# Normalising the mixer input half by half, putting an attention head first, and planning the issue order with other durations, in a fused decoder layer

## The chip, the cores and the metric

The program runs on one core of a Trainium2 chip. The metric is device time in microseconds (us) of one execution; lower is better. The core has five engines with in-order instruction queues: TensorE (PE in the profile, with its weight loads as PEld), VectorE (DVE), ScalarE (ACT), GpSimd (POOL) and SyncE (SP, which here only issues DMAs). They meet only through semaphores. A measurement of this kernel can tell a change from none at about 0.5% of its time.

## What is computed

One inference step of a hybrid decoder layer on 544 tokens (512 of a prompt, 32 of eight samples), width 1024, in float32:

```python
x = x + 0.5 * swiglu(rms(x, norm_ffn1))                  # feed-forward block 1
h = rms(x, norm_mix)                                     # the mixer input
qa, ka, va, qkv_b, z_b, b_b, a_b, gate = split(h @ w_in) # one wide projection
o_a = merged_attention(qa, ka, va)                       # 12 heads in 3 groups (dilation 1, 4, 16)
o_b = gated_deltanet(qkv_b, z_b, b_b, a_b)               # 8 heads, conv of width 4, chunked delta rule
gt  = sigmoid(gate)
x = x + (gt_a * (o_a @ w_proj_a) + gt_b * (o_b @ w_proj_b)) @ w_out
x = x + 0.5 * swiglu(rms(x, norm_ffn2))                  # feed-forward block 2
y = rms(x, norm_out)
```

`rms(x, w) = x * rsqrt(mean(x*x) + 1e-6) * w`. Keys, values, conv rows and delta-net states are outputs too.

## The kernel before

**Layout and units.** Activations lie transposed: 8 tiles of 128 features by 544 tokens. Tokens are worked in two halves of 272, called h = 0 and 1. The work on PE is a list of *units* (`make_plan`, L155). A unit is one column block of a weight matrix times one half: for the wide projection 8 weight tiles, and for each three matmuls of 128x272, since a float32 product is made of split halves: weight-high x input-high, weight-high x input-low, weight-low x input-high (`unit`, L612). So a unit of the mixer has 24 matmuls. The split of the input is a pair of tiles named `xh` and `xl`, that of a weight group `G`.

**The mixer's order.** After feed-forward block 1 come two units `ba`, then the list `MIX_ORDER` (L43): `("p", k)` is delta-net head k (query, key, value: 6 units), `("a", k)` an attention head (6 units), `z` the delta-net's output gate (2 units each), `t` the branch gates (4 units each). After the list come the projections `pa` and `pb`.

**The norm factor.** The mixer's input needs a factor r per token that is known only after the whole of x is known and ACT and POOL have summed its squares. The kernel starts the mixer without it: the first units multiply x times the norm weight, without r, and each result is multiplied by r when DVE takes it out of PSUM (`take`, L870). Meanwhile a generator `renorm` (L561) makes normalised tiles `xn2` for all 544 tokens: per tile one DVE multiply (name `xt`), one ACT copy (`xh`), one DVE subtraction (`xl`). From unit `first_ba + NORMED` on (L38, L687) the units use these, and ACT takes their results out of PSUM. `renorm` is started when the second half's factor is there (`norm_fin`, L601).

**Side work and the planner.** All that is not a unit (conv, the delta-net pair of heads `gdn_pair`, its sample part, attention per slot `attn_slot`, `attn_sample`, `z_fin`, `fin_a`, the norm) is a Python generator. While the program is written, `pump` (L646) runs after every third matmul of a unit and lets each generator go on for one step if the planner's clock says its operands are there. That clock is `Meter` (L48): it adds up an assumed duration for each recorded instruction, engine by engine and for the DMA queue (L75 to L93). Nothing of this runs on the chip; it fixes only the order in each engine's queue. When a unit needs something that is not there yet (a buffer, a conv before it, a loaded tile), `until` and `force` (L292, L666) run side work alone until it is. The names that matter below: `ob`, the delta-net output of a head, stored to DRAM (`od`) and loaded again for `z_fin` (L824); `oad` and `oA`, the attention output stored and loaded again by `fin_a` (L849) for `pa`; `av`, an attention head's projected values; `g`, the decay of the delta-net, made by `gating` (L954), with `gc`, `gm` and `LB`/`LA` beside it; `convout`, the conv states, loaded at the start of the mixer (L774).

Of the kernel before, what the change touches and what calls it, by code (L numbers as in the profile page):

```python
# [37 lines left out]
NORMED = 10  # L38
# [4 lines left out]
MIX_ORDER = [("p", 0), ("p", 1), ("a", 0), ("p", 2), ("a", 1), ("p", 3), ("a", 2), ("a", 3), ("p", 4), ("a", 4), ("p", 5), ("a", 5)]  # L43
# [4 lines left out]
class Meter:  # L48
# [10 lines left out]
    def note(self, eng, op, args, kw):  # L59
# [201 lines left out]
class Builder:  # L261
# [299 lines left out]
    def renorm(self):  # L561

        ts = []

        def finish():
            t, (hi, lo) = ts.pop(0), self.xn2[-1 - len(ts)]
            self.tt(lo, t, hi, ALU.subtract)
            self.free(1)

        for n in range(KT):  # L570
            yield from self.need(3)
            t = self.S(name="xt")
            self.stt(t, self.x[n], self.wn[1][:, n:n + 1], self.rr, ALU.mult, ALU.mult)
            if ts:
                finish()
            yield "scalar"
            self.xn2.append((self.S(dt=F32R, name="xh"), self.S(dt=F32R, name="xl")))
            self.act(self.xn2[-1][0], t, AF.Copy)
            ts.append(t)
            t = None  # L580
            yield "vector"
        finish()
        self.renormed = True

    def norm_fin(self, h):
# [15 lines left out]
        elif h == 1 and self.in_mix:  # L601
            self.spawn(self.renorm())
# [77 lines left out]
    def kernel_units(self):  # L680
# [4 lines left out]
        first_ba = next(i for i, u in enumerate(self.units) if u[0] == "ba")  # L685
        for ui, u in enumerate(self.units):
            self.prefetch(ui)  # L687
            if ui == first_ba + NORMED:
                self.until(lambda: self.renormed)
                self.xn, self.xn2, self.normed = self.xn2, None, True  # L690
                self.free(2 * KT)
# [78 lines left out]
    def enter_mix(self):  # L770
# [5 lines left out]
        self.xn2, self.renormed, self.normed = [], False, False  # L776
        self.live = 16 + 1 + 2 + KT
# [18 lines left out]

    def u_ba(self, h, wids):
# [8 lines left out]
    def u_z(self, n, h, wids):  # L806
# [4 lines left out]
        ps, s = self.unit(wids, self.xn, h), self.sl(h)  # L811
# [1026 lines left out]
```

## Time and profile before

| | us |
|---|---|
| three timed runs | 1721.02, 1719.72, 1713.33 (median 1719.72) |
| the profiled execution | 1718.26 |
| its span, first to last instruction | 1716.5 |
| PE busy / DVE busy / ACT busy | 1648.8 / 1010.2 / 618.8 |

The span has three parts: feed-forward block 1 to about 414 us, the mixer to about 1280 us, feed-forward block 2 to the end. A timeline row gives start, duration, engine, operation, written tile and read tiles, and in brackets the idle time of the engine before it with what ended it. Matmuls overlap: what counts is the distance of their starts. "PEclk" is the granted TensorE clock as a share of full speed: 1.00 stands for 2.4 GHz, 0.50 for 1.2 GHz.

### The profile page before, as it was taken

The page shows a single profiled execution, that of the slowest core. Times are in us where ns is not written, and L with a number is a line of the kernel's source. Part 1 is how long each engine was busy: PE and PEld are TensorE (multiplying, and loading weights), DVE is VectorE, ACT ScalarE, POOL GpSimd, SP SyncE. Part 2 cuts the span into 40 slices and gives each one's busy share as a digit, 9 for nine tenths or more (in the row PEclk, how much of TensorE's full clock was granted, in tenths as well). Part 3 has the DMA queues.
Part 4 walks back from the last instruction along what each step waited for, and adds up shares of the span by engine and source line. Part 5 has one row for each costly group of instructions (what it writes and reads, how often), then busy time and mean ns, then how long its engine had stood idle before and what let it go on. Part 6 is the DMA issues. An engine that isn't in the chain of part 4 may idle for free.

```text
span 1716.5 us, 33595 instructions
## 1 busy us (share of the span) xinstructions
PE 1648.8 (96%) x13373; PEld 1603.2 (93%) x13373; DVE 1010.2 (59%) x2460; ACT 618.8 (36%) x1548; POOL 169.0 (10%) x289
## 2 busy tenths in 40 slices
PE   7999999999699998998999979999999999999997
PEld 7999999999599978997999978999999999999997
DVE  7754255545867857876866566353356654255534
ACT  5332232332344424553433425332233332223332
POOL 5000000011111211221021111000011000000012
PEclk9999999999899999998999979999999999999999
DMA  5223222221334454564445756433242223223221
GB/s 178 86 87 99 86 83 90 87 81 58 125 99 141 150 185 119 176 199 128 160 151 180 253 160 193 142 111 90 94 140 88 87 87 93 92 75 99 87 75 65
DMA packets 116433, 205.12 MB, mean 120 GB/s; under 512 B 30962, under 2 KB 57108, under 8 KB 116276
## 3 DMA queue, kind: packets, MB, share of 16 engines
q1 hardware_dynamic: 104708, 162.43, 29.7%
q0 software_dynamic: 10992, 39.99, 7.8%
q8 instruction: 105, 1.72, 0.4%
q10 hardware_dynamic: 576, 0.56, 0.1%
q14 instruction: 52, 0.43, 0.1%
HBM read 172.20 MB, written 30.73 MB: 118 GB/s over the span
## 4 chain that ended last, share of the span: by engine, by line
PE 85%; DVE 7%; DMA 4%; ACT 1%; issue 1%; SPq 0%; DVEq 0%; POOL 0%; ACTq 0%
PE mm L122 43%; PE sd L122 42%; DVE R L122 1%; DMA md<-ast 1%; DVE H L122 1%; DVE y L122 1%; DMA ob<-od 1%; DVE G L122 1%; DMA st<-in_ssm_dram 1%; DVE xl L122 1%; DVE r L122 1%; DMA cache<-in_kc_dram 0%; ACT s L122 0%; SPq L122 0%; DMA raw<-in_W_dram 0%
## 5 line engine op out<-in xcount | busy, mean ns | idle before, releaser
L122 PE MATMUL mm<-xh,G 128*128 128x272 f32 x3632 | 744.3, 296 | 9.0 <-ACT xh L122 3.1
L122 PEld LDWEIGHTS mm<-xh,G 128*128 128x128 f32 x3632 | 590.8, 191 | 27.8 <-issue 13.2
L122 PE MATMUL mm<-xl,G 128*128 128x272 f32 x1816 | 527.6, 291 | 8.5 <-DVE xl L122 8.5
L122 DVE TENSOR_TENSOR G<-raw,G 128x512 fp32r<-128x512 f32 x468 | 303.9, 691 | 180.3 <-ACT G L122 174.7
L122 PE MATMUL sd<-xh,G 128*128 128x272 f32 x1904 | 362.5, 288 | 0.0
L122 PEld LDWEIGHTS mm<-xl,G 128*128 128x128 f32 x1816 | 347.0, 191 | 10.5 <-DVE xl L122 9.8
L122 ACT ACTIVATE G<-raw 128x512 fp32r<-128x512 f32 x474 | 272.1, 622 | 101.5 <-PE mm L122 47.3
L122 PEld LDWEIGHTS sd<-xh,G 128*128 128x128 f32 x1904 | 300.2, 188 | 0.2
L122 PE MATMUL sd<-xl,G 128*128 128x272 f32 x952 | 273.6, 287 | 0.0
L122 PEld LDWEIGHTS sd<-xl,G 128*128 128x128 f32 x952 | 179.0, 188 | 0.1
L122 PE MATMUL sd<-hh,G 128*128 128x272 f32 x1287 | 163.2, 288 | 0.0
L122 PEld LDWEIGHTS sd<-hh,G 128*128 128x128 f32 x1287 | 161.9, 188 | 0.1
L122 POOL TENSOR_TENSOR acc<-acc,H 128x272 f32<-128x272 f32 x55 | 44.5, 810 | 909.9 <-ACT H L122 908.9
L122 ACT ACTIVATE hh<-H 128x272 fp32r<-128x272 f32 x88 | 38.0, 432 | 201.8 <-DVE H L122 201.8
L122 PE MATMUL mm<-hh,G 128*128 128x272 f32 x825 | 104.7, 288 | 0.0
L122 PEld LDWEIGHTS mm<-hh,G 128*128 128x128 f32 x825 | 103.8, 188 | 0.0
L122 ACT ACTIVATE H<-H 128x272 f32<-128x272 f32 (+1 forms) x89 | 38.2, 429 | 161.2 <-DVE H L122 161.2
L122 POOL DMA_DIRECT2D raw<-in_W_dram x76 | 41.7, 549 | 519.9 <-DVE G L122 283.1
L122 DVE SCALAR_TENSOR_TENSOR H<-H,H 128x272 f32<-128x272 f32 x120 | 55.7, 465 | 30.7 <-ACT H L122 30.2
L122 DVE SCALAR_TENSOR_TENSOR x<-sd,x 128x272 f32<-128x272 f32 x49 | 21.5, 439 | 78.2 <-PE sd L122 78.2
L122 DVE TENSOR_TENSOR hh<-H,hh 128x272 fp32r<-128x272 f32 x88 | 39.0, 443 | 43.8 <-ACT hh L122 43.8
L122 DVE SCALAR_TENSOR_TENSOR y<-U,vec,y 128x568 f32<-128x568 f32 x72 | 62.1, 863 | 3.8 <-ACT y L122 1.9
(261 smaller groups left out, 1763.2 us busy)
## 6 DMA issues: line engine op xcount, KB each, us to landing
raw<-in_W_dram SPq DMA_DIRECT2D x161, 512.0 KB, 3.5
raw<-in_W_dram POOLq DMA_DIRECT2D x76, 512.0 KB, 4.2
qkv<-qd SPq DMA_DIRECT2D x36, 256.0 KB, 5.0
st<-in_ssm_dram SPq DMA_DIRECT2D x32, 256.0 KB, 4.8
cache<-in_kc_dram SPq DMA_DIRECT2D x28, 256.0 KB, 3.8
cache<-in_vc_dram SPq DMA_DIRECT2D x28, 256.0 KB, 4.5
qd<-av SPq DMA_DIRECT2D x24, 256.0 KB, 3.0
out_dram<-av SPq DMA_DIRECT2D x24, 256.0 KB, 3.1
```

Source lines behind the costliest of these rows:

```text
L122: r = f(*args, **kw)
```

## The change

The mixer input is normalised in halves: `renorm(h)` is started as soon as that half's factor is there, works on 128x272, and units switch to the normalised tiles for half 0 from unit 8 and for half 1 from unit 9 (before: both from 10). `MIX_ORDER` begins with an attention head, `("a", 0)`, which stood third. `Meter` gets other numbers: DMA issue to start 1.6 for 1.1 us and 250 for 358 GB/s, a matmul 0.011 + 0.00042 for 0.00043 us per column, 0.2 us more for an ACT operation with an accumulator. `z_fin` now gives up its turn until the planner's clock says that `ob` is loaded.

```diff
-NORMED = 10
+NORMED = (8, 9)
...
-MIX_ORDER = [("p", 0), ("p", 1), ("a", 0), ("p", 2), ("a", 1), ...
+MIX_ORDER = [("a", 0), ("p", 0), ("p", 1), ("p", 2), ("a", 1), ...
...
-            self.t["dma"] = max(self.t["dma"], self.t[eng] + (1.1 if eng == "sync" else 0.65)) + size / 358
+            self.t["dma"] = max(self.t["dma"], self.t[eng] + (1.6 if eng == "sync" else 0.65)) + size / 250
...
-                c = 0.11 if op == "transpose" else (n * 0.00043 if r.dtype == F32R else
+                c = 0.11 if op == "transpose" else (0.011 + n * 0.00042 if r.dtype == F32R else
...
-                c = 0.12 + n / 1400
+                c = 0.12 + n / 1400 + (0.2 if "accum_out" in kw else 0.0)
...
-    def renorm(self):
+    def renorm(self, h):
+
+        s = self.sl(h)
+        last = None
         for n in range(KT):
-            yield from self.need(3)
-            t = self.S(name="xt")
-            self.stt(t, self.x[n], self.wn[1][:, n:n + 1], self.rr, ALU.mult, ALU.mult)
-            if ts:
-                finish()
+            t = self.H()
+            self.stt(t, self.x[n][:, s], self.wn[1][:, n:n + 1], self.r[h], ALU.mult, ALU.mult)
+            if last:
+                self.tt(*last, ALU.subtract)
             yield "scalar"
...
+            hi, lo = self.xn2[n]
+            self.act(hi[:, s], t, AF.Copy)
+            last = (lo[:, s], t, hi[:, s])
             yield "vector"
+        self.tt(*last, ALU.subtract)
+        self.normed[h] = True
...
-        elif h == 1 and self.in_mix:
-            self.spawn(self.renorm())
+        elif self.norm_no == 1:
+            self.spawn(self.renorm(h))
...
+            for k in range(2):
+                if ui == first_ba + NORMED[k]:
+                    self.until(lambda: self.normed[k])
+                    self.use[k] = True
...
-        self.live = 16 + 1 + 2 + KT
+        self.live = 32 + 1 + 2 + KT
...
+    def xm(self, h):
+        return self.xn2 if self.use[h] else self.xn
...
         self.stt(z, t, 1.0, z, ALU.add, ALU.mult)
+        yield self.ob[n]
         self.tt(z, z, self.ob[n][:, s], ALU.mult)
```

The units of `z`, `gdn`, `at` and `gate` take `self.xm(h)` where they took `self.xn`, and `take` goes by `self.use[h]`.

What this does to the queues is shown at three places. Numbers in names count tiles; rows are in the order of issue.

*First place, the start of the mixer, on DVE.* Before, once the second `ba` result (`bas`) is out of PSUM:

```order
L122 TENSOR_TENSOR G_4729<-raw_4452,G_4729 128x512
L122 TENSOR_TENSOR G_4732<-raw_4452,G_4732 128x512
L122 MEMSET U_4760 128x3
L122 COPY U_4760<-convout_4652 128x8x3
L122 TENSOR_TENSOR U_4760<-mm_4735,r_4632 128x272
L122 SCALAR_TENSOR_TENSOR xt_4768<-x_71,vec_79,r_4632 128x544
L122 COPY LB_4778<-sd_4773 128x32
L122 COPY LA_4779<-sd_4773 128x32
```

After, at the same place (five rows of the half 0 normalisation already stand ahead of it, before the second half's factor is made):

```order
L122 TENSOR_TENSOR G_4746<-raw_4452,G_4746 128x512
L122 TENSOR_TENSOR G_4749<-raw_4452,G_4749 128x512
L122 TENSOR_TENSOR av_4777<-mm_4752,r_4632 128x272
L122 SCALAR_TENSOR_TENSOR H_4783<-x_74,vec_79,r_4632 128x272
L122 TENSOR_TENSOR xl_4744<-H_4723,xh_4743 128x272
L122 SCALAR_TENSOR_TENSOR H_4786<-x_71,vec_79,r_4632 128x272
L122 COPY LB_4796<-sd_4791 128x32
L122 COPY LA_4797<-sd_4791 128x32
```

The copy out of `convout` no longer stands ahead of the normalisation (it comes 51 rows further on), and the two halves' rows are mixed.

*The same stretch on PE*, around the matmuls that read `g`. Before, they stand near the end of the first unit that reads normalised tiles:

```order
L122 MATMUL mm_633_5128<-xh_626_5111,G_608_4999 128x272
L122 MATMUL sd_635_5161<-g_634_5151,mats_10_80 128x32
L122 MATMUL sd_635_5161<-g_634_5151,mats_10_80 128x2
L122 MATMUL sd_635_5161<-g_634_5151,mats_10_80 128x32
L122 MATMUL sd_635_5161<-g_634_5151,mats_10_80 128x2
L122 MATMUL mm_633_5128<-xh_631_5124,G_608_4999 128x272
L122 MATMUL mm_633_5128<-xl_632_5125,G_608_4999 128x272
```

After, they stand 18 matmuls into the second such unit (`mm_630`), and the first one (`mm_625`) has the transposes of `av` after its ninth matmul:

```order
L122 MATMUL mm_625_5035<-xl_570_4744,G_612_4949 128x272
L122 MATMUL mm_625_5035<-xh_569_4743,G_612_4949 128x272
L122 MATMUL sd_626_5046<-mats_10_80,av_618_4988 128x128 x4
L122 MATMUL mm_625_5035<-xh_583_4815,G_612_4949 128x272
L122 MATMUL mm_625_5035<-xl_584_4816,G_612_4949 128x272
```

So PE meets two things made by DVE in these units beside the tiles: `av` and `g`.

*Second place, the first `z` units, on DVE.* Before:

```order
L122 SCALAR_TENSOR_TENSOR H_1852_12118<-H_1853_12119,H_1852_12118 128x272
L122 TENSOR_TENSOR H_1852_12118<-H_1852_12118,ob_1847_12077 128x272
L122 SCALAR_TENSOR_TENSOR H_1856_12152<-H_1857_12153,H_1856_12152 128x272
L122 TENSOR_TENSOR H_1856_12152<-H_1856_12152,ob_1847_12077 128x272
L122 TENSOR_TENSOR Y_1806_11825<-Y_1806_11825,sd_1867_12210 128x8x32
L122 STREAM_TRANSPOSE X_1836_12041<-Y_1806_11825 32x4x32
```

After:

```order
L122 SCALAR_TENSOR_TENSOR H_1812_12003<-H_1813_12004,H_1812_12003 128x272
L122 TENSOR_TENSOR inv_1817_12017<-Yc_1699_11376,Uc_1698_11375 128x136
L122 TENSOR_TENSOR Yc_1699_11376<-Yc_1699_11376,inv_1817_12017 128x8x17
...
L122 TENSOR_TENSOR Yc_1699_11376<-Yc_1699_11376,inv_1826_12055 128x8x14
L122 TENSOR_TENSOR H_1812_12003<-H_1812_12003,ob_1782_11881 128x272
L122 TENSOR_TENSOR inv_1829_12075<-Yc_1699_11376,Uc_1698_11375 128x104
```

The multiply that reads `ob` stood right behind the one before it and ahead of the delta-net's `Y` and `X`; now twelve rows lie between.

*Third place, the end of the mixer, on SP.* Before, the last attention output is stored and loaded long before the projections; the loads of the last two heads' `ob` stand after the second to fourth of them:

```order
L122 DMA oad_554_4660<-o_2060_13170 128x512
L122 DMA oA_2071_13231<-oad_554_4660 128x512
...
L122 DMA oA_2083_13319<-oad_554_4660 128x512
...
L122 DMA oA_2092_13378<-oad_554_4660 128x512
L122 DMA oA_2101_13438<-oad_554_4660 128x512
```

After, they come last of all side work, behind those `ob` loads:

```order
L122 DMA ob_2122_13714<-ods_553_4659 128x32
L122 DMA oad_554_4660<-o_2127_13747 128x512
L122 DMA oA_2138_13807<-oad_554_4660 128x512
L122 DMA oA_2157_13913<-oad_554_4660 128x512
L122 DMA oA_2160_13922<-oad_554_4660 128x512
L122 DMA oA_2163_13928<-oad_554_4660 128x512
```

On PE the last matmuls of that attention output are followed by 60 unit matmuls before the first one of `pa`; before, by more than 400.

## Rows read from the trace of the kernel before

**Rows 1.** The page's part 1: engine, busy us, share of the span, instructions.
```profile
PE 1648.8 (96%) x13373; PEld 1603.2 (93%) x13373; DVE 1010.2 (59%) x2460; ACT 618.8 (36%) x1548; POOL 169.0 (10%) x289
```
**Rows 2.** Windows by stage: stretch, its length, then busy us and count of PE, PEld, DVE, ACT, POOL, the granted TensorE clock, the DMA share and GB/s.
```profile
37.00:414.00 377.00, 376.91 (x3001) 376.91 (x3002) 199.03 (x396) 116.80 (x241) 10.05 (x13) 1.00 0.27 86
414.00:480.00 66.00, 49.78 (x326) 45.49 (x325) 46.85 (x122) 20.22 (x42) 8.17 (x15) 0.84 0.26 84
...
600.00:670.00 70.00, 61.87 (x623) 52.93 (x622) 47.05 (x162) 22.83 (x66) 7.75 (x20) 0.93 0.49 159
...
765.00:820.00 55.00, 48.84 (x387) 41.11 (x386) 38.28 (x103) 22.96 (x63) 10.62 (x22) 0.91 0.53 165
...
980.00:1010.00 30.00, 19.35 (x159) 17.48 (x158) 16.09 (x48) 9.45 (x32) 5.34 (x7) 0.66 0.71 214
1010.00:1062.00 52.00, 49.21 (x416) 45.61 (x418) 32.05 (x103) 25.86 (x81) 6.28 (x11) 0.97 0.66 194
1062.00:1280.00 218.00, 218.00 (x1794) 214.51 (x1783) 97.07 (x202) 78.10 (x177) 10.79 (x18) 1.00 0.36 116
```
**Rows 3.** Timeline of PE at the start of the mixer, from the first matmul of `ba` to the last of the twelfth unit.
```profile
414.13 0.49 PE L122 MATMUL mm<-xh,G 128*128 128x272 f32 x1
...
426.22 0.31 PE L122 MATMUL sd<-mats,bas 40*128 40x40 f32 x2 [0.88 <-DVE bas L122]
...
455.77 0.39 PE L122 MATMUL mm<-xh,G 128*128 128x272 f32 x1 [1.80 <-ACT xh L122]
460.69 0.59 PE L122 MATMUL mm<-xl,G 128*128 128x272 f32 x1 [4.53 <-DVE xl L122]
...
467.40 0.60 PE L122 MATMUL mm<-xl,G 128*128 128x272 f32 x1 [2.80 <-DVE xl L122]
...
469.80 1.87 PE L122 MATMUL sd<-g,mats 128*128 128x32 f32 x8 [1.57 <-DVE g L122]
...
479.89 0.29 PE L122 MATMUL mm<-xh,G 128*128 128x272 f32 x1
```
**Rows 4.** Timeline of DVE in the same stretch.
```profile
425.74 0.43 DVE L122 TENSOR_TENSOR bas<-mm,r 40x272 f32<-40x272 f32 x1
426.09 1.28 DVE L122 TENSOR_TENSOR G<-raw,G 128x512 fp32r<-128x512 f32 x2
...
432.43 0.18 DVE L122 COPY U<-convout 128x24 f32<-128x24 f32 x1 [5.05 <-DMA convout<-in_convst_dram]
432.52 0.43 DVE L122 TENSOR_TENSOR U<-mm,r 128x272 f32<-128x272 f32 x1
432.87 0.78 DVE L122 SCALAR_TENSOR_TENSOR xt<-x,vec,r 128x544 f32<-128x544 f32 x1
433.57 0.18 DVE L122 COPY LB<-sd 128x32 f32<-128x32 f32 x1
...
436.89 2.50 DVE L122 SCALAR_TENSOR_TENSOR y<-U,vec,y 128x568 f32<-128x568 f32 x3
...
445.01 0.72 DVE L122 TENSOR_TENSOR xl<-xt,xh 128x544 fp32r<-128x544 f32 x1
```
**Rows 5.** Waits of PE in the mixer (413 to 1280 us): waiting engine and tile, what ended the wait, total us, times, longest.
```profile
PE mm L122 <- DVE xl L122: 8.5, 5, 4.5
PE sd L122 <- DVE X L122: 8.4, 2, 8.0
...
PE sd L122 <- DVE srz L122: 4.4, 2, 2.4
PE sd L122 <- DMA cache<-in_kc_dram: 4.4, 2, 2.8
...
PE sd L122 <- DMA st<-in_ssm_dram: 2.2, 1, 2.2
```
**Rows 6.** Timeline of PE at the first `z` units.
```profile
987.10 2.05 PE L122 MATMUL sd<-Y,Pm 128*128 128x64 f32 x16 [1.09 <-DVE Pm L122]
...
997.71 1.94 PE L122 MATMUL sd<-X,B 128*64 128x64 f32 x16 [8.03 <-DVE X L122]
```
**Rows 7.** Timeline of DVE there.
```profile
995.63 0.44 DVE L122 TENSOR_TENSOR H<-H,ob 128x272 f32<-128x272 f32 x1 [4.74 <-DMA ob<-od]
```
**Rows 8.** The chain that ended last, there: start, us, what.
```profile
983.62 11.91 DMA ob<-od
```
**Rows 9.** Windows right behind four waits of PE, PE alone: stretch, length, PE busy and count, granted clock, DMA share, GB/s.
```profile
457.00:477.00 20.00, 10.49 (x40) 0.50 0.09 27
...
662.00:668.00 6.00, 6.00 (x27) 0.50 0.80 264
...
998.00:1009.00 11.00, 9.47 (x70) 0.50 0.62 169
1057.00:1061.00 4.00, 3.85 (x19) 0.57 1.07 340
```
**Rows 10.** The tile `o` (an attention output): its instructions with min/median/max ns and first and last start, and how long its DMA took to land.
```profile
L122 DVE TENSOR_TENSOR o<-o,sd x4: 1082/1097/1130, 739.1 to 1076.0; 128x512 f32<-128x512 f32 x4
...
DMA to landing us min/median/max: 2.0/2.4/4.1
```
**Rows 11.** The same view of the tile `oA`.
```profile
L122 ACT ACTIVATE oh<-oA x4: 621/624/627, 1082.8 to 1102.1; 128x512 fp32r<-128x512 f32 x4
L122 DVE TENSOR_TENSOR ol<-oA,oh x4: 684/693/694, 1083.4 to 1102.9; 128x512 fp32r<-128x512 f32 x4
...
DMA to landing us min/median/max: 2.7/3.8/5.0
```

More of the change, by code (lines that the diff above doesn't have):

```diff
@@ L559, in xw_tile @@
         self.stt(lo[:, s], self.x[n][:, s], w, hi[:, s], ALU.mult, ALU.subtract)
[L561 to L580 removed]
+    def renorm(self, h):
+        s = self.sl(h)
+        last = None
+        for n in range(KT):
+            t = self.H()
+            self.stt(t, self.x[n][:, s], self.wn[1][:, n:n + 1], self.r[h], ALU.mult, ALU.mult)
+            if last:
+                self.tt(*last, ALU.subtract)
+            yield "scalar"
+            if h == 0:
+                self.xn2.append((self.S(dt=F32R, name="xh"), self.S(dt=F32R, name="xl")))
+            hi, lo = self.xn2[n]
+            self.act(hi[:, s], t, AF.Copy)
+            last = (lo[:, s], t, hi[:, s])
             yield "vector"
[L582 to L583 removed]
+        self.tt(*last, ALU.subtract)
+        self.normed[h] = True
     def norm_fin(self, h):
@@ L600, in norm_fin @@
             self.store_y(h)
-        elif h == 1 and self.in_mix:
-            self.spawn(self.renorm())
+        elif self.norm_no == 1:
+            self.spawn(self.renorm(h))
+        if h == 1:
+            self.norm_no += 1
     def store_y(self, h):
@@ L685, in kernel_units @@
         first_ba = next(i for i, u in enumerate(self.units) if u[0] == "ba")
+        self.xn2, self.normed = [], [False, False]
+        self.use, self.norm_no = [False, False], 0
         for ui, u in enumerate(self.units):
             self.prefetch(ui)
[L688 to L691, printed above, removed]
+            for k in range(2):
+                if ui == first_ba + NORMED[k]:
+                    self.until(lambda: self.normed[k])
+                    self.use[k] = True
+                    if self.use[1 - k]:
+                        self.xn = self.xn2
+                        self.free(2 * KT)
             pend.append(getattr(self, "u_" + u[0])(*u[1:]))
@@ L810, in u_z @@
                 self.z_load(n + 1)
-        ps, s = self.unit(wids, self.xn, h), self.sl(h)
+        ps, s = self.unit(wids, self.xm(h), h), self.sl(h)
         def evac():
@@ L877, in u_gdn @@
     def u_gdn(self, hd, t, h, wids):
-        nc, done = self.nc, self.normed
-        ps = self.unit(wids, self.xn, h)
+        nc, done = self.nc, self.use[h]
+        ps = self.unit(wids, self.xm(h), h)
         def evac():
@@ L945, in spill @@
         self.xd = self.D([P, KT, NT], "xd")
-        while not self.renormed:
+        while not all(self.normed):
             yield "w"
@@ L1407, in u_at @@
     def u_at(self, j, g, t, h, wids):
-        nc, A, done = self.nc, self.A, self.normed
-        ps = self.unit(wids, self.xn, h)
+        nc, A, done = self.nc, self.A, self.use[h]
+        ps = self.unit(wids, self.xm(h), h)
         def evac():
@@ L1691, in u_gate @@
     def u_gate(self, n, ab, h, wids):
-        ps = self.unit(wids, self.xn, h)
+        ps = self.unit(wids, self.xm(h), h)
         def evac():
@@ L1730, in evac @@
             if (n, h) == (7, 1):
-                self.xn = self.oAs = self.oBs = None
+                self.xn = self.xn2 = self.oAs = self.oBs = None
                 self.x = [self.S(name="x") for _ in range(KT)]
```

3 lines of the change are left out of this document (1 added, 2 removed).

## The prediction, made before the result was known

> **What bounds the kernel now.** I read the page's part 1 first. PE is busy for 96% of the span and no other engine for more than 59% [rows 1], so the time changes only where PE waits, where its clock falls, or where it gets more to do. The change adds no matmul. The windows by stage come next [rows 2]: feed-forward block 1 has PE busy for all of its 377 us, and 1062 to 1280 us, the end of the mixer, for all of its 218. A matmul of 128x272 thus costs 377/3001 = 0.1256 us at full clock. What can be gained lies between 414 and 1062 us, in five places that [rows 2] shows: the entry (66.0 us, clock 0.84), 600 to 670 us (8.1 idle, 0.93), 765 to 820 (6.2 idle, 0.91), the first `z` units (30.0 us, 0.66), and 1010 to 1062 (2.8 idle). The waits tell who is late [rows 5]: `xl` at the entry (8.5 us), `X` (8.4), `srz` (4.4), and two loads, `cache` (4.4) and `st` (2.2). Last come the windows behind four waits: where PE had waited, it then ran for 4 to some 20 us at half the clock, though busy for all or most of it [rows 9]. So a wait of 4 us here costs its length and, after it, half of the busy time at 0.50.
>
> All sums are made against the profiled execution: 1718.26 us, of which 1716.5 is the span and 1.8 lies outside; it is 1.5 below the median of the runs.
>
> **A. The entry.** The first `ba` matmul starts at 414.13 and the last of the twelfth unit at 479.89 [rows 3]: with the last matmul 65.9 us. Twelve units are 288 matmuls, 36.2 us at 0.1256; the other 38 of the 326 in this window are small and I give them 2. PE loses 27.7 us: 11.6 in the waits that [rows 3] shows (0.88, 1.80, 4.53, 2.80, 1.57), and most of the rest at half clock (457 to 477: 10.49 busy at 0.50, [rows 9]).
>
> Why `xl` is late stands in [rows 4]. DVE is done with `G` at 426.09 + 1.28 = 427.4, then waits 5.05 us for the DMA of `convout`, because a small copy stands ahead of the first `xt` (432.87). After that the conv, 2.50 us for three `y` rows, goes between the tiles. The change takes both away: the copy comes 51 rows later, and with the attention head first there is no conv yet.
>
> The working of DVE after: 5 rows of half 0 go ahead of this point, about 1.9 us, so it goes on at 429.3. To the last `xl` tile of half 0 stand 20 normalising rows, two `G` pairs (2 x 1.28), six evacuations and nine small rows. A row of 272 elements takes 0.43 alone but 0.35 from start to start (432.52 to 432.87), one of 544 takes 0.70 so (432.87 to 433.57) and 0.72 to 0.78 alone [rows 4]. With 0.35: 7.0 + 2.6 + 1.6 + 1.8 = 13.0; with 0.44 for the 20 rows 14.8. The last tile is there at 442.3 to 444.1. PE needs it some 28 us of work (eight units, 24.1, the two small products and about 0.9 of waiting for `bas`, plus most of the ninth unit) after 414.1, at about 442.9: a stall of 0 to 1.2 us. But the first unit with normalised tiles has the transposes of `av` after nine matmuls (first place of the order), about 440.6, and DVE takes that `av` out of PSUM behind the tiles, at about 444.1. I count a wait of 4 us (3.5 to 5.4), half clock for 6 us behind it, so 3 more [rows 9] (662 to 668), 0.8 at the matmuls that read `g` (they stand 18 matmuls into the next unit and were 1.57 late before), and 1.2 of the smaller waits, `bas` among them: 9 lost instead of 27.7. **A = -18.7** (bounds: loss 5 to 15, so -12 to -23). That half 1 switches one unit after half 0 costs nothing if its rows, mixed with those of half 0, end within 3 us of them.
>
> The Trainium skill has a rule against cutting rows in two ("VectorE: DVE Perf Modes", "The TRN2 errata"): an operation out of SBUF carries a fixed latency beside its elements, by its formula (N+151)/0.96 ns, 0.44 us for 272 elements and 0.72 for 544. The trace agrees in the durations (0.43 and 0.72, [rows 4]), not in the distance of starts (0.35 and 0.70). By the page 32 halves for 16 wholes are 2.6 us more of DVE, by the starts none; A would be about -17 by the page.
>
> **B. The multiply that reads `ob`.** Before, DVE waits 4.74 us on it [rows 7]; the DMA had taken 11.91 in the chain [rows 8]; `Y` and `X` stand behind it, so PE waits 8.03 for `X`, after 1.09 for `Pm` [rows 6], and then runs 9.47 us at half clock [rows 9] (998 to 1009), 4.7 lost. Together 13.8. After, twelve rows of DVE lie between (second place) and 56 unit matmuls, 7.0 us of PE, so the wait of 4.74 has cover. This goes: **B = -13.8** (bounds -13.8 to 0). What is late next: in the order a run of side products without unit matmuls remains at the start of `z`, 17 in place of 28; I leave **+4** for it (0 to +8.5, 17/28 of 13.8).
>
> **C. Buffers at heads 4 and 6.** The first delta-net pair now starts six attention units later, 6 x 24 x 0.1256 = 18.1 us, while heads 2 and on stand where they stood. Units of heads 4 and 6 need buffers that earlier pairs free, and side work runs alone until then. In the order these runs grow from 28 to 40 groups of rows on PE (head 4) and from 18 to 22 (head 6). They lie in 600 to 670 and 765 to 820: 8.1 and 6.2 idle [rows 2], `srz` among it. In proportion: 8.1 x 40/28 = 11.6 and 6.2 x 22/18 = 7.6, **C = +5** (bounds -5, if side work that is better spread waits less, to +20).
>
> **D. Waits on loads.** `cache` 4.4 and `st` 2.2 [rows 5], and half clock behind one of them (1057 to 1061: 3.85 busy at 0.57, [rows 9], 1.5 lost): 8. The planner now gives a DMA 0.5 us more to start and 43% more per byte, so such steps are let go later. Half of it, **D = -4** (bounds -8 to 0).
>
> **E. The end of the mixer.** Here PE never waited [rows 2] (1062 to 1280). After, the store of `o` and the loads of `oA` come last on SP (third place), with 60 unit matmuls, 7.5 us, between the last product of that output and `pa`. The chain: `o` 1.10, landing 2.4 [rows 10], landing of `oA` 3.8, `oh` 0.62, one `ol` 0.69 [rows 11], two other DVE rows in between at no more than `o`'s 1.1 each, 2.2, and an estimate of 0.2 for the hand-overs: 11.0 in all. PE lacks 11.0 - 7.5 = 3.5, and runs at half clock behind it as in A, 2.5. **E = +6** (bounds 0, if the landings are 2.0 and 2.7 and other side products fill the rest, to +10, with 4.1 and 5.0).
>
> For this the Trainium skill states ("DMA: Bandwidth & Descriptors", "Anatomy of one DMA") for transfers that GpSimd issues a fixed cost of about 2 us each, most of it the receipt of the write, and 436 GB/s beside it. A store and the load that depends on it pay that twice: about 5.2 us, an estimate by that page with 0.6 each for 128x512 floats; here SP issues them. The trace has 2.4 + 3.8 = 6.2 [rows 10, 11]; by the page E would be about +5.
>
> **F.** PE changes between unit and side matmuls 190 times in place of 178; no row prices a change; between nothing and a whole matmul (0.1256) each, 12 cost 0 to 1.5, and I take the upper part, **+1**.
>
> Sum: -18.7 - 13.8 + 4 + 5 - 4 + 6 + 1 = -20.5, and 1718.3 - 20.5 = 1697.8. I say **1698**.
>
> **Rivals.**
> 1. *The planner's numbers are worth more than I think.* It now counts 0.125 us for a matmul of 272 columns where it counted 0.117, and the trace has 0.1256 [rows 2]; with such numbers side work stops stalling: nothing is left at `z`, C is 0 and D whole. -18.7 - 13.8 - 8 + 4 (E smaller) + 1 = -35.5: 1683. For it: `cache` and `st` waits are those of a planner that believes loads are early. Against it: the waits on `srz` and `X` come from forced runs, which no duration removes.
> 2. *Only the entry gains.* The `ob` wait is replaced by one of the same length on another product of the chain, since z units come only when the last pair is still at work. B and its +4 give nothing: -18.7 + 5 - 4 + 6 + 1 = -10.7, and with C at twice my value about -6: 1708 to 1712, say 1711.
> 3. *Slower: the delta-net comes too late.* The 18.1 us by which the first pair starts later are not made up; heads 4 and 6 both wait for their buffers by that much, each with 3 of clock behind it: C = 42. -18.7 - 13.8 + 4 - 4 + 6 + 1 + 42 = +16.5: 1735. It decides against the change from C above 25.5. For it: both runs grow in the order. Against it: they grow by 12 and 4 groups, not by the six units' worth.
> 4. *The change does not do what it says at the entry.* DVE stays the bound, half 1 ends long after half 0, and the stall moves from the eleventh unit to the tenth: half of A, 1707. For it: the same elements go through DVE, in twice the instructions.
>
> **Chances.** Forecast 0.57 (own range 1688 to 1708, from A's and C's bounds taken together), rival 1 0.15, rival 2 0.15, rival 3 0.08, rival 4 0.05. The range 1682 to 1714 takes in rivals 1, 2 and 4 and leaves out the third and tails of the first two, some 0.18. A measurement of this kernel tells about 0.5%, 8.6 us, from no change: faster is below 1711.1, slower above 1728.3 against the median. Faster: nearly all of the forecast (0.55), rival 1 (0.15), a good third of rival 2 (0.06), half of rival 4 and more (0.03): 0.79. Slower: 0.08 from rival 3. The rest, 0.13, is the same.
>
> **What would show it.** In the trace after: no DVE wait on `convout` ahead of the normalised tiles; the twelfth unit ends some 46 to 49 us after the first `ba` matmul, with `av` as the longest wait of PE; no DVE wait on `ob` and no 8 us wait on `X` at the first `z` units; PE idle near heads 4 and 6 of some 19 us; a wait of PE on `oh` or `ol` at the first `pa`. I am wrong if the entry still takes over 55 us, if C passes 20, or if another wait of over 5 us stands where the one on `X` stood.

## The result and the profile after

| | before | after |
|---|---|---|
| median of the runs, us | 1719.58 (1713.33 to 1721.02) | 1705.22 (1704.77 to 1707.67) |
| the profiled execution, us | 1718.26 | 1707.67 |
| its span, us | 1716.5 | 1705.8 |

The ratio is 0.9929, 95% interval 0.9912 to 0.9946: faster by 0.7%. It is taken over all the runs of both kernels and is not the quotient of the two medians (0.9916), so a difference between two kernels below is known to some 3 us. Two executions in all, one of the kernel before and one of the last variant, took 2006 and 7107 us and enter no ratio. The forecast was 1698; the range of 1682 to 1714 holds the result. The sum behind it did not come out term by term, and that is what the experiments are about.

The page's part 1 of the kernel after, against [rows 1]: the same work on PE, 10.7 us less span.

```profile
PE 1646.0 (96%) x13373; PEld 1604.1 (94%) x13373; DVE 1012.1 (59%) x2473; ACT 620.8 (36%) x1559; POOL 165.5 (10%) x289
```

Windows by stage of the kernel after, columns as in [rows 2]:

```profile
414.00:480.00 66.00, 61.75 (x484) 60.36 (x483) 51.05 (x138) 27.68 (x68) 5.87 (x16) 1.00 0.42 136
480.00:600.00 120.00, 116.00 (x901) 115.11 (x901) 96.23 (x278) 53.25 (x172) 22.50 (x48) 0.97 0.40 120
600.00:700.00 100.00, 99.51 (x963) 92.05 (x962) 75.11 (x225) 44.38 (x123) 14.98 (x39) 1.00 0.55 174
700.00:840.00 140.00, 131.58 (x1112) 124.30 (x1112) 91.94 (x276) 65.79 (x207) 25.36 (x45) 0.98 0.58 170
840.00:960.00 120.00, 114.11 (x1026) 102.58 (x1025) 84.79 (x266) 40.51 (x131) 21.28 (x38) 0.97 0.64 196
960.00:1062.00 102.00, 92.93 (x802) 85.56 (x802) 64.75 (x203) 46.63 (x137) 14.38 (x26) 0.95 0.55 172
1062.00:1280.00 218.00, 209.41 (x1638) 207.56 (x1638) 101.16 (x215) 75.96 (x176) 10.22 (x15) 0.98 0.35 107
```

The same stretches of the kernel before that [rows 2] does not have:

```profile
480.00:600.00 120.00, 119.77 (x954) 119.13 (x953) 95.06 (x274) 54.32 (x176) 23.20 (x48) 1.00 0.45 140
600.00:700.00 100.00, 91.86 (x863) 82.78 (x862) 70.39 (x220) 38.50 (x109) 14.09 (x32) 0.95 0.54 171
700.00:840.00 140.00, 131.68 (x1085) 121.05 (x1085) 102.91 (x299) 64.59 (x198) 23.99 (x45) 0.96 0.52 156
840.00:960.00 120.00, 119.55 (x1092) 111.91 (x1090) 86.11 (x295) 51.80 (x168) 21.77 (x45) 1.00 0.53 168
960.00:1062.00 102.00, 88.56 (x736) 82.24 (x736) 57.51 (x168) 39.85 (x122) 13.73 (x22) 0.88 0.69 208
```

Length minus PE's busy time is what PE stood still. Three stretches improved: the entry (16.2 to 4.3 us idle), 600 to 700 (8.1 to 0.5), and 960 to 1062 (13.4 to 9.1). Three got worse, and all of these had been full before: 480 to 600 (0.2 to 4.0), 840 to 960 (0.5 to 5.9), and 1062 to 1280 (0.0 to 8.6). The time lost to a fallen clock can be counted too: in windows of 5 us from 410 to 1290 us, idle time plus busy time times (1 - PEclk) comes to 66.7 us before and 54.8 after. This sum is called the *loss* below. The difference, 11.9, less the 1.0 us by which the first `ba` matmul started later, is the 10.7 of the span within 0.2.

Who is late now, waits of PE from 413 to 1280 us, against [rows 5]:

```profile
PE sd L122 <- ACT vk L122: 9.1, 1, 9.1
PE sd L122 <- DMA cache<-in_kc_dram: 5.4, 1, 5.4
PE sd L122 <- ACT av L122: 5.0, 3, 4.0
PE sd L122 <- DVE s L122: 4.0, 2, 3.1
PE sd L122 <- ACT oh L122: 2.9, 2, 2.4
...
PE mm L122 <- DVE G L122: 1.8, 1, 1.8
```

`xl` and `srz`, 12.9 us together before, are nearly gone (0.4 and 0.8). In place of the 8.0 us for `X` at the first `z` units stands one wait of 9.1 for `vk`.

PE at the entry, timeline of the kernel after, against [rows 3]:

```profile
415.09 0.49 PE L122 MATMUL mm<-xh,G 128*128 128x272 f32 x1
...
428.54 0.31 PE L122 MATMUL sd<-mats,bas 40*128 40x40 f32 x2 [2.24 <-DVE bas L122]
445.11 0.44 PE L122 MATMUL sd<-mats,av 128*128 128x128 f32 x2 [0.26 <-DVE av L122]
446.29 0.44 PE L122 MATMUL sd<-mats,av 128*128 128x128 f32 x2 [0.75 <-DVE av L122]
451.45 1.05 PE L122 MATMUL sd<-g,mats 128*128 128x32 f32 x8 [0.60 <-DVE g L122]
...
459.03 0.41 PE L122 MATMUL mm<-xh,G 128*128 128x272 f32 x2
```

The last row holds the end of the twelfth unit, at 459.44: the entry took 44.4 us, at full clock throughout. Counted the same way, unit matmul by unit matmul (12 x 24 = 288), the twelfth unit before ended at 477.67, so its entry was 63.5 us. The row at 479.89 that [rows 3] gives for it belongs to the unit after; the prediction's 65.9 was 2.4 too long.

### The profile page after: what moved, and what is told of

It reads as the page before. It is cut to its first block, busy times and chain, and to the rows that moved or that the text cites. A ratio compares the mean times of both kernels' runs of the same rounds, so it can differ in the third digit from the quotient of the medians.

```text
span 1705.8 us, 33626 instructions
## 1 busy us (share of the span) xinstructions
PE 1646.0 (96%) x13373; PEld 1604.1 (94%) x13373; DVE 1012.1 (59%) x2473; ACT 620.8 (36%) x1559; POOL 165.5 (10%) x289
## 4 chain that ended last, share of the span: by engine, by line
PE 81%; DVE 9%; DMA 5%; ACT 3%; issue 2%; SPq 1%; DVEq 0%; ACTq 0%
PE sd L122 42%; PE mm L122 39%; DMA md<-ast 3%; DVE H L122 1%; DVE G L122 1%; DVE inv L122 1%; DVE y L122 1%; ACT s L122 1%; SPq L122 1%; DMA ast<-md 1%; DVE Yc L122 1%; DVE R L122 1%; DVE nrm L122 1%; DVE xl L122 0%; ACT G L122 0%
```

## The experiments

The change has four parts that can be had one without the other: the attention head first (order), the normalisation by halves (halves), the planner's new durations (numbers), and the new turn in `z_fin` (turn). Eight kernels take them apart; four more test what was late after. All times are medians of timed runs, all ratios are to the kernel before on the same chip at the same time; the last row was timed apart from the others, beside 1719.6 us of the kernel before. "Entry" is from the first `ba` matmul to the end of the twelfth unit, counted in the timeline; the idle columns are PE's, in us, from windows.

| run | parts | us | ratio (95%) | entry | idle 600-700 | 840-960 | 960-1062 | 1062-1280 |
| --- | --- | --- | --- | --- | --- | --- | --- | --- |
| before | none | 1720.8 | 1 | 63.5 | 8.1 | 0.5 | 13.4 | 0.0 |
| order_only | order | 1717.4 | 0.9988 (0.9976 to 0.9999) | 42.7 | 14.7 | 1.7 | 21.5 | 0.0 |
| halves_only | halves | 1721.0 | 1.0006 (0.9995 to 1.0017) | 63.6 | 6.0 | 0.5 | 15.2 | 0.0 |
| numbers_only | numbers | 1716.4 | 0.9978 (0.9959 to 0.9997) | 64.4 | 0.1 | 6.2 | 4.3 | 8.4 |
| z_turn_only | turn | 1718.0 | 0.9985 (0.9970 to 1.0001) | 63.7 | 5.9 | 0.6 | 9.5 | 0.0 |
| halves_and_order | halves, order | 1721.6 | 1.0011 (0.9997 to 1.0025) | 47.0 | 15.3 | 1.7 | 20.1 | 0.0 |
| order_and_numbers | order, numbers | 1714.4 | 0.9966 (0.9952 to 0.9980) | 42.8 | 0.6 | 6.2 | 17.9 | 4.4 |
| old_numbers | halves, order, turn | 1715.1 | 0.9967 (0.9950 to 0.9985) | 48.5 | 14.2 | 1.8 | 11.3 | 0.0 |
| without_z_turn | halves, order, numbers | 1713.6 | 0.9962 (0.9948 to 0.9976) | 45.1 | 1.7 | 6.5 | 18.3 | 4.8 |
| after | all four | 1705.2 | 0.9929 (0.9912 to 0.9946) | 44.4 | 0.5 | 5.9 | 9.1 | 8.6 |

Since work shifts between stretches when a part is changed, an idle column says where PE stood at that time, not always at the same work. Two columns follow one part: every kernel with the new numbers has some 6 us idle from 840 to 960 us and 4 to 9 from 1062 on, and every kernel with the old ones has under 2 there.

**Order alone, halves alone.**

```diff
-MIX_ORDER = [("p", 0), ("p", 1), ("a", 0), ("p", 2), ("a", 1), ("p", 3), ("a", 2), ("a", 3), ("p", 4), ("a", 4), ("p", 5), ("a", 5)]
+MIX_ORDER = [("a", 0), ("p", 0), ("p", 1), ("p", 2), ("a", 1), ("p", 3), ("a", 2), ("a", 3), ("p", 4), ("a", 4), ("p", 5), ("a", 5)]
```

> The kernel before with the attention head first alone; the normalisation stays whole and units switch at the tenth. Theory 1: the conv and the wait for its states no longer stand ahead of the normalised tiles, which are finished 5 us earlier for the wait and some 5 for the conv; the entry is 8 to 12 us shorter than before (54 to 58 us), 1708 to 1714 us. Rival: DVE has as much to do before the last xl tile, and the entry gains only the 5.05 us of the wait: 1713 to 1717.

> The kernel before with the normalisation by halves alone; the delta-net heads stay first, units switch at the eighth and ninth. Theory 1: the halves start early enough that most of the rows of half 0 stand ahead of the conv copy, but the conv rows (2.5 us for three y) and the wait on convout still fall between; the entry is 3 to 10 us shorter, 1709 to 1717. Rival: units now need the tiles two units (6 us) sooner and DVE is no faster, so the entry is as long as before or longer: 1717 to 1724.

`halves_only` is the new `renorm(h)` with `NORMED = (8, 9)` in the kernel before. The order alone shortens the entry by 21 us, twice what theory 1 expected, and the rival's bound of 5 falls. The halves alone shorten it by nothing, as their rival had it: DVE waits for `convout` as it did, 5.82 us now, with the tiles behind it (timeline of DVE, halves_only):

```profile
435.83 0.18 DVE L122 COPY U<-convout 128x24 f32<-128x24 f32 x1 [5.82 <-DMA convout<-in_convst_dram]
...
436.27 0.49 DVE L122 SCALAR_TENSOR_TENSOR H<-x,vec,r 128x272 f32<-128x272 f32 x1
```

Yet `order_only` ends only 3.4 us sooner. The windows of that run show where the rest went:

```profile
600.00:700.00 100.00, 85.30 (x796) 75.43 (x796) 67.99 (x210) 37.41 (x107) 13.01 (x35) 0.90 0.46 137
...
960.00:1062.00 102.00, 80.51 (x672) 73.47 (x671) 54.29 (x164) 44.35 (x134) 10.48 (x18) 0.88 0.67 180
```

PE stands 14.7 and 21.5 us there, 14.7 more than before in the two together, and one wait at the first `z` units is longer than any of before (waits of PE, order_only):

```profile
PE sd L122 <- DVE St L122: 13.7, 2, 12.6
```

This fits the prediction's third rival, the delta-net that starts six units later, at less than half its price of 42 us; for the whole change it was wrong.

**Halves and order; numbers alone.** `halves_and_order` is the whole change without the numbers and the turn; `numbers_only` changes these lines of the kernel before:

```diff
-            self.t["dma"] = max(self.t["dma"], self.t[eng] + (1.1 if eng == "sync" else 0.65)) + size / 358
+            self.t["dma"] = max(self.t["dma"], self.t[eng] + (1.6 if eng == "sync" else 0.65)) + size / 250
...
-                c = 0.11 if op == "transpose" else (n * 0.00043 if r.dtype == F32R else
+                c = 0.11 if op == "transpose" else (0.011 + n * 0.00042 if r.dtype == F32R else
...
-                c = 0.12 + n / 1400
+                c = 0.12 + n / 1400 + (0.2 if "accum_out" in kw else 0.0)
```

> The normalisation by halves and the attention head first, with the planner's old numbers and without the new turn in z_fin. Theory 1 (the entry gives about 21 us in the kernel after, and what the new numbers and the new turn moved later on gave back about 9 of it): the twelfth unit ends 44 to 47 us after the first ba matmul, and the whole takes 1697 to 1704 us, less than the 1705.2 of the whole change. Theory 2 (the new numbers gain too, and the 9 us are the price of the later delta-net start): the entry is the same, but the loads are waited for as before, DVE waits 4 us or more on ob at the first z units, and the whole takes 1708 to 1716.

> The kernel before with the planner's new numbers alone. Theory 1: the waits are dealt out anew but not fewer; 1714 to 1726 us, the entry still 64 to 67 us long. Theory 2: the waits on loads (cache 4.4, st 2.2) and part of the stall at z go, 1703 to 1712 us.

Theory 1, that the entry carries the gain and the rest costs, fell with the first: a short entry, and no gain at all (1721.6). Theory 2 had the direction there but not the size (1708 to 1716). For `numbers_only` it was theory 1 that held: 1716.4, in its range of 1714 to 1726 and not in 1703 to 1712. The two windows from 600 to 670 us, numbers_only and then old_numbers (below), show what the numbers do there:

```profile
600.00:670.00 70.00, 69.92 (x696) 61.92 (x694) 53.35 (x168) 30.74 (x85) 11.18 (x23) 1.00 0.51 158
```
```profile
600.00:670.00 70.00, 55.81 (x471) 48.58 (x470) 49.72 (x157) 24.37 (x74) 8.03 (x20) 0.80 0.39 120
```

With the new numbers PE has 0.1 us of idle time there, at full clock, here and in the kernel after, so whichever head comes first. With the old ones and the attention head first it stands 14.2 us and runs at a mean clock of 0.80 (the kernel before: 8.1 us). PE comes to this place in the same state: at 600 us `order_only` has done 53.8 units and 108 other matmuls, `order_and_numbers` 53.1 and 104. In the next 50 us the first does 1.3 units beside 236 other matmuls, the second 10.1 beside 202: with the old numbers the delta-net's products stand there with hardly a unit between them. Which of the new durations changes this was not tried.

Further on the numbers cost. In `numbers_only` PE stands in two stretches that were full before (119.55 of 120 and 218.00 of 218 us busy):

```profile
840.00:960.00 120.00, 113.80 (x1011) 104.11 (x1010) 85.93 (x273) 37.92 (x107) 27.30 (x47) 0.97 0.65 207
...
1062.00:1280.00 218.00, 209.56 (x1650) 208.77 (x1649) 96.52 (x199) 74.55 (x173) 9.42 (x16) 0.98 0.35 108
```

**Three of the four.**

> The kernel before with the attention head first and the planner's new numbers; the normalisation stays whole, no turn in z_fin. Theory 3 (new, from the four runs: the order alone shortens the entry by 20 us, the later delta-net start gives it back between 600 and 660 us and at the first z units, and only the new numbers keep the gain; the halves bring nothing): entry 43 to 46 us, no wait of over 3 us between 600 and 660, 1702 to 1710 us. Rival (the halves are needed with it): 1713 to 1720.

> The whole change with the planner's old numbers. Theory 3: the entry keeps its 44 to 47 us, the stalls between 600 and 660 us are back (10 us and more, with the clock at half behind them), 1714 to 1722 us. Rival (the turn in z_fin is what keeps the gain): 1704 to 1710.

> The whole change without the new turn in z_fin. Theory 3: the turn matters only at the z units; DVE waits on ob there again, for 3 to 6 us, and 1704 to 1712 us. Rival (the turn moved the wait, it did not remove it): the same as the whole change within 2 us, 1703 to 1707, with PE idle for about as long at the first z units.

`order_and_numbers` against `without_z_turn` differ by the halves alone: 1714.4 and 1713.6, intervals that overlap almost wholly. The halves brought nothing that these runs can tell; at the entry they cost 2 us (42.8 to 45.1) and 4 with the old numbers (42.7 to 47.0), where the whole kernel is 4 us slower with them as well (1717.4 to 1721.6). Of this 1.3 us is `bas`, 2.2 us late instead of 0.9: five of their rows stand ahead of the second half's factor. Theory 3 had put `order_and_numbers` at 1702 to 1710, as good as the whole change, and missed that: the turn was needed. Its 1714.4 lies in the rival's range, but not for the rival's reason, as the halves do not help. `old_numbers` fits theory 3 (1715.1, 14.2 us idle from 600 to 700). `without_z_turn` came out above both expectations: the whole change gains 6 us (by the ratios) to 8 us (by the medians) by the turn. It is not the wait on `ob` that the turn takes away there. DVE waits 13.1 us for `ob` in `order_only`, and nearly as long in `halves_and_order` (its waits of DVE from 955 to 1065 us):

```profile
DVE H L122 <- DMA ob<-od: 12.2, 1, 12.2
```

In `without_z_turn`, `order_and_numbers` and `numbers_only` it does not wait for it at all: the new numbers alone bring that. What PE has more in `without_z_turn` than in the kernel after, beside 10.0 us for `vk` (9.1 after), is 4.2 us for `zm`, a tile of GpSimd. On the kernel before the turn gains less:

```diff
         self.stt(z, t, 1.0, z, ALU.add, ALU.mult)
+        yield self.ob[n]
         self.tt(z, z, self.ob[n][:, s], ALU.mult)
```

> The kernel before with the new turn in z_fin alone. The prediction's step B priced it at -13.8 + 4, that is 1708 to 1712 us, with no wait of over 3 us at the first z units. Theory 3, as the run without the turn left it: the multiply no longer blocks DVE, but PE's next product of the last delta-net pair is late all the same, so a wait of 5 us or more stands at another product there (vk, r or St), and the gain is 2 to 8 us: 1712 to 1718.

Neither side holds fully. The wait on `X` shrank from 8.03 to 2.67 us and no wait of 5 us took its place, as step B had it, but the kernel gained 2.8 us, with an interval that includes nothing at all. PE stood 3.9 us less from 960 to 1062, and 2.6 more from 700 to 840 (10.9 for 8.3). Up to the first `z` units the two kernels have the same order on every engine, so those 2.6 are what two executions of one order differ by, and idle columns that differ by less than some 3 us tell nothing. Single parts add up to 3.4 - 0.2 + 4.4 + 2.8 = 10.4 us, all together gave 14.4 (by the ratios 7.4 and 12.2). What the order is worth within the whole change stays open: numbers and turn without the order were not run. Under the new numbers alone it is worth 2.0 us (1716.4 to 1714.4).

**The wait at the first z units.** In the kernel after, the timeline of ACT and then of DVE ahead of PE's product of `vk` at 986.45 (9.07 us late):

```profile
983.43 0.75 ACT L122 ACTIVATE oh<-H 128x272 fp32r<-128x272 f32 x2 [3.85 <-DVE H L122]
...
984.96 1.15 ACT L122 ACTIVATE G<-raw 128x512 fp32r<-128x512 f32 x2
986.00 1.28 ACT L122 ACTIVATE vk<-vk,nrmk 128x128 f32<-128x128 f32 x4
```
```profile
974.82 0.16 DVE L122 TENSOR_SCALAR nrm<-os 128x8 f32<-128x8 f32 x1
...
984.79 0.16 DVE L122 TENSOR_TENSOR nrmk<-nrm,nrmk 128x8 f32<-128x8 f32 x1
```

From the first `nrm` (a row of the delta-net pair's norm factor) to `nrmk` (its last) there are 10 us in which DVE is hardly ever idle (11.35 of 12.00 us busy from 974 to 986): the small rows of the factor stand between rows of the sample part, of `z_fin` and of the weights. By these rows PE and ACT wait for DVE's queue, not for `ob`. If that is so, work for PE that asks little of DVE covers it; the gate units have one ACT operation each:

```diff
-MIX_ORDER += [("z", n) for n in range(6)] + [("t", n) for n in range(4)] + [("z", n) for n in (6, 7)]
+MIX_ORDER += [("t", n) for n in range(4)] + [("z", n) for n in range(8)]
```

> The whole change with the branch gates ahead of all z units in the order list (16 units, 48 us of PE, between the last attention head and the first z). If the wait of 9.07 us on vk at the first z units comes from the last delta-net pair still being at work when z begins, the gates cover it: no wait over 3 us there, the half clock behind it goes too, 1690 to 1698 us. Rival (DVE is the bound there, and what is moved ahead of it only moves the wait): a wait of 6 us or more stands at the gates or at the later z units, 1702 to 1712.

1697.2 us, ratio 0.9865 (0.9847 to 0.9884): 8 us faster than the kernel after by the medians, 11 by the ratios. The windows show no wait at all in that place, and then one where the kernel after has none (52.00 of 52 us busy at full clock):

```profile
960.00:1010.00 50.00, 50.00 (x453) 46.00 (x446) 33.34 (x112) 16.99 (x43) 12.65 (x22) 1.00 0.65 204
1010.00:1062.00 52.00, 45.07 (x364) 41.28 (x363) 26.79 (x87) 25.72 (x85) 1.34 (x3) 0.90 0.52 131
```

The rival is out by its own condition, since no wait of 6 us stands at the gates or behind: the longest is 3.85 us, on a load of `cache`, then 1.74 on `r`. But it is not out as a mechanism. From 960 to 1065 the loss is 10.7 us, where the kernel after lost 11.3; what shrank is the loss from 840 to 960 (9.0 to 3.5) and at the end of the mixer (12.6 to 7.5). Whether the waits from 1010 on are the old one in another place was not tried; in the last kernel below a wait of 3.2 us for `vk` stands at 1042 us.

**Two other waits, on this kernel.** The first is the one for `cache` at 756 us:

```diff
         for i in range(2):
             self.dma(lay[i](md[i]), fl(X[:, 0, i], i))
+        yield md
...
-            end = self.t["dma"] + 0.9
+            end = self.t["dma"] + 0.9 + (9.0 if name(outs[0]).startswith("md") else 0.0)
```

> The kernel gates_before_z, where attention now gives up its turn between the store of md and its reload ast, and the planner counts 9 us more for that store (the trace after has 12 us from the store's issue to its landing, with SyncE standing at the reload and the loads of cache behind it). Theory: the wait of PE on cache at 756 us (6.0) is SyncE's wait at that reload, not a slow load; it goes, with the half clock behind it, and 1687 to 1694 us. Rival: the load itself is late, since the planner lets it go late; the wait stays at 4 us or more and the time at 1695 to 1699.

1691.2 us, ratio 0.9829 (0.9800 to 0.9857): in the range of the theory, and the theory is wrong. The wait on `cache` is still there, 6.64 us. SP issues the load right behind the store now, at 738.45 (timeline of SP):

```profile
736.01 2.34 SPq L122 DMA_DIRECT2D md<-ast  x2
738.45 0.42 SPq L122 DMA_DIRECT2D cache<-in_kc_dram  x1
```

but it landed 13.4 us later, where such loads take 4.4 in the median of this run. Windows of the same run show a DMA system that moves almost nothing meanwhile:

```profile
738.00:740.00 2.00, 2.00 (x15) 1.11 (x11) 1.18 (x5) 1.93 (x8) 0.16 (x2) 1.00 0.00 0
...
744.00:746.00 2.00, 1.25 (x10) 1.03 (x9) 1.93 (x3) 0.00 (x0) 1.31 (x2) 1.00 0.28 25
```

0 to 45 GB/s until 748, then 261 and more. GpSimd's load of 512 KB, issued at 736.25 between the two stores, took 15.3 us where the median is 4.2, so loads of both queues were held up, and they landed together with the second store, within 0.2 us of 751.67. So neither theory nor rival: the load was late although SP no longer stood at the reload (11.7 us in the kernel after). That the store itself holds them up is read from this one place. The gain came later; there SP waited less for such stores, which may be its cause. Its waits from 800 to 1110 us, gates_before_z and then reload_apart:

```profile
SPq L122 <- DMA md<-ast: 29.8, 3, 10.4
```
```profile
SPq L122 <- DMA md<-ast: 8.9, 3, 8.1
```

The second edit concerns GpSimd:

```diff
-            self.tt(vk[h], vk[h], bc(ki[:, i * 4:i * 4 + 4]), ALU.mult, pg)
-            self.tt(kn[h], kn[h], bc(c1[:, i * 4:i * 4 + 4]), ALU.mult, pg)
+            self.tt(vk[h], vk[h], bc(ki[:, i * 4:i * 4 + 4]), ALU.mult)
+            self.tt(kn[h], kn[h], bc(c1[:, i * 4:i * 4 + 4]), ALU.mult)
```

> The kernel gates_before_z with the four multiplies of vk and kn by nrmk of each delta-net pair on VectorE in place of GpSimd. In the trace after one DVE multiply R<-R,gc,mats takes 4.59 us where the others take 0.34, while GpSimd does those four (4.2 us). Theory: DVE stands still while GpSimd's tensor_tensor runs; on DVE the four cost 4 x 0.69 = 2.8 us and R comes some 1.5 us earlier, so PE's wait of 4.0 us on av at 528 shrinks to 2 to 3 us and no R takes over 1 us; 1692 to 1697 us. Rival: the long R is a wait for an operand that the record puts into its duration; R stays as late, DVE has 11 us more to do in all, 1697 to 1703.

The rows of the tile `R` in the kernel after and in scale_on_vector (count, min/median/max ns, first and last start):

```profile
L122 DVE SCALAR_TENSOR_TENSOR R<-R,gc,mats x32: 337/344/4585, 521.7 to 886.0; 128x128 f32<-128x128 f32 x32
```
```profile
L122 DVE SCALAR_TENSOR_TENSOR R<-R,gc,mats x32: 342/344/351, 523.7 to 850.3; 128x128 f32<-128x128 f32 x32
```

1685.5 us, ratio 0.9795 (0.9771 to 0.9819), faster than the theory expected. No `R` takes over 0.351 us, and the wait of 4.0 us on `av` at 528 shrank to 0.3. That direct part, with the half clock behind it, is 6.5 - 0.6 = 5.9 us by the 5 us windows from 480 to 600; the rest of the 11.8 us against gates_before_z lies further on, mostly at the end of the mixer (7.5 to 0.0 from 1062 to 1290), where the planner dealt the waits anew. Why just those went was not tried. Both edits together:

> The kernel gates_before_z with both edits, the reload of md apart from its store and the multiplies of vk and kn on VectorE. If the two gains add, 1685.5 - 6.0 = 1679 us (1676 to 1683). Rival (every edit that the planner sees deals the later waits anew, and the two take away the same ones): 1684 to 1690, with other waits of PE in place of those that went.

1681.2 us (the median of three runs), ratio 0.9759 (0.9733 to 0.9784): inside the range where the gains add. This version beats both kernels (the one after has 0.9929 against the same). Its page's part 1:

```profile
PE 1638.4 (98%) x13373; PEld 1596.0 (95%) x13373; DVE 1007.8 (60%) x2489; ACT 619.5 (37%) x1559; POOL 147.4 (9%) x273
```

## Why the prediction was right, and where its steps were not

**A, the entry: right in size and in the wait that goes, not in which edit takes it away.** Forecast -18.7; the entry went from 63.5 to 44.4 us, -19.1. Both ends were off by about the same: by the prediction's own count it lost 25.3 us before, not 27.7 (the misread row), and 6.2 after, not 9, because the wait for `av` was 1.0 us in two pieces and not 4, with the clock at 1.00 behind it. (That count puts the small matmuls at 2 us. By the windows the loss was 21.6 and 4.3, 17.3 less, which leaves 4 to 6 us for them.) The prediction named the wait on `convout` and the conv ahead of the tiles, and priced the halves with them without separating the two edits. The runs do: it is the order, 20.8 us alone; the halves add a wait on `bas` instead. DVE no longer waits for `convout` among the tiles; its two waits there, 1.23 us and 0.56, are for `beta` and `g` (its timeline, kernel after, against [rows 4]):

```profile
429.96 0.48 DVE L122 SCALAR_TENSOR_TENSOR H<-x,vec,r 128x272 f32<-128x272 f32 x1
430.37 0.42 DVE L122 TENSOR_TENSOR xl<-H,xh 128x272 fp32r<-128x272 f32 x1
430.72 0.48 DVE L122 SCALAR_TENSOR_TENSOR H<-x,vec,r 128x272 f32<-128x272 f32 x1
```

A multiply of 272 elements takes 0.41 us from start to start and a subtraction 0.35: between the 0.35 that the sum took and the 0.44 by the rule of the Trainium skill that the prediction weighed ("VectorE: DVE Perf Modes", "The TRN2 errata"), nearer to the sum. But the prediction set a subtraction's 0.35 against the 0.70 of a multiply of 544. In the kernel before a subtraction of 544 takes 0.64 (440.44 to 441.08). So a pair of halves costs 0.06 us more than the whole for a subtraction and 0.12 for a multiply, about 1.4 us for the eight tiles where the prediction had none. It decided nothing.

**B, the multiply that reads `ob`: what it removes was right, that little follows was not.** DVE does not wait for `ob` any more, which the new numbers bring without the turn as well. But PE's 13.8 us (8.03 + 1.09 + 4.7) became 11.4: 9.07 for `vk`, and 2.3 at half clock (5.55 busy at 0.59 from 986 to 992). That is rival 2's mechanism, at its place; step B left 4 for it. The prediction named a wait of over 5 us in the place of `X` as a sign of being wrong, and that sign is there. In the stage as a whole (960 to 1062) the loss still fell by 8.7, near B's 9.8 net.

**C, the buffers at heads 4 and 6: the wrong sign.** Forecast +5. The two windows, 14.3 us idle before, have 1.6 after (70.00 - 69.91 and 55.00 - 53.50). I counted rows without unit matmuls in the order and took their number for time. `order_only` shows what I feared (14.7 idle from 600 to 700), and under the new numbers it is gone. The prediction gave the numbers only **D**, -4 for half of two waits on loads; those went from 4.4 + 2.2 to 5.4. The loss from 600 to 840 fell by 13.4 us (24.5 to 11.1), where C and D made +1.

**E, the end of the mixer: right in size.** Forecast 3.5 of wait and 2.5 of clock; measured 2.39 + 0.65 + 0.51 = 3.55 for `oh` and `ol` and 2.5 at half clock (timeline and window of PE, kernel after):

```profile
1121.17 0.59 PE L122 MATMUL sd<-oh,G 128*128 128x272 f32 x1 [2.39 <-ACT oh L122]
1122.41 0.59 PE L122 MATMUL sd<-ol,G 128*128 128x272 f32 x1 [0.65 <-DVE ol L122]
```
```profile
1121.00:1128.00 7.00, 5.54 (x21) 0.54 0.20 75
```

The table of runs adds what the step did not see: PE stands in this stretch under the new numbers alone (8.4 us in `numbers_only`, 2.3 and 0.9 of them for `oh` and `ol`) and in no kernel with the old ones.

**F, the changes between unit and side matmuls.** The loss accounts for the span within 0.2 us, so nothing of the +1 shows.

**What no step priced** is the 21 us in stretches that had been full: `av` at 528 (4.0 and 2.4 of clock), `r` and others from 840 to 960 (5.9 and 3.1, less 0.5 before), and `G` and `s` ahead of the projections (5.0 and 1.5). The runs say where these come from: the first from the order (3.1 us for `av` in `order_only`, no wait from 480 to 600 in `numbers_only`), the others from the numbers (6.2 and 8.4 us idle in `numbers_only`, 1.7 and 0.0 in `order_only`). The 14 us by which 600 to 840 came out better than C and D pay for two thirds of it, and the total came out 7 us above the forecast, still inside its range. That the errors of 21 and 14 us cancel to this degree is luck. The failing step is the sum itself: it priced the places where the order visibly changed, left the rest of a re-planned order as it was, and took what a place gains for what the kernel gains. A's -18.7 came true at the entry, but the order that brings it is worth 3.4 us to the kernel alone and 2.0 under the new numbers. Of the rivals the first (the numbers are worth more) was right for 600 to 840 us, the second at `z`; the measured time lies between them.

## What to carry to other kernels

When a planner writes the order, a gain at one place is not yet a gain of the kernel: the attention head first took 21 us off the entry and 3 off the kernel, and the rest came back as waits further on. Better durations did the same: they emptied one stretch of waits and put others into two that had been full. Price a re-planned order from the stretches that are full as well as from those that wait, and give it a term of its own. When a wait goes away, look for the chain that the same engine still has to finish there; work for PE that asks little of that engine, put in front of it, gave 8 us here on top of the edit to the wait itself, though other waits stood further on afterwards.

## What the runs showed of the hardware

**A DVE row with two tiles as inputs stood still while GpSimd multiplied.** In the kernel after GpSimd does four multiplies without a break (timeline of POOL), while one `R` of DVE, 0.34 us in the median, takes 4.59:

```profile
521.85 1.08 POOL L122 TENSOR_TENSOR vk<-vk,nrmk 128x512 f32<-128x512 f32 x1 [0.54 <-DVE nrmk L122]
...
524.99 1.08 POOL L122 TENSOR_TENSOR kn<-kn,nrmk 128x512 f32<-128x512 f32 x1
```

It ends when they end; with these on DVE (0.69 each) it is gone. The Trainium skill has this ("SBUF — State Buffer", "Who interferes with whom"): a DVE operation with two inputs in SBUF and a GpSimd operation that reads SBUF exclude each other for the whole instruction. The trace agrees, and adds that one DVE row can sit out four GpSimd rows in a run. The kernel before has the same long row; I had not looked at a maximum beside a median.

**Stores of 4 KB in small pieces took 8 to 14 us to land, and loads issued around one landed with it.** `md` is stored by two transfers, one in pieces of 4 bytes and one in pieces of 16. The trace of reload_apart has the landing of two of them, 13.7 and 11.9 us after the issue; the kernel before has three, 7.7 to 10.7, the kernel after one, 12.2. The reloads of the same bytes took 4.6 and 6.2 in reload_apart. The load of `cache` issued behind the first pair took 13.4 us, and GpSimd's load of 512 KB issued between the two took 15.3. What makes one of these stores slower than another stays open.
